# A weight block's low part: from a VectorE subtraction to ScalarE's negation and an accumulating DMA

## The chip, the cores and the metric

The kernel runs on one core of one Trainium2 chip. The metric is the device time of one execution in microseconds, the median of several runs. The core's engines are TensorE (PE in the profile; PEld is its weight load), VectorE (DVE), ScalarE (ACT), GpSimd (POOL) and SyncE (SP, which here only issues DMAs). Each engine works through its own queue in order and waits on semaphores for the others. A DMA that an engine issues stands in that engine's queue like any instruction: what it waits for holds back what is queued behind it.

## The reference

One inference step of a streaming encoder layer: an adaLN-modulated norm, an input projection, banded softmax attention beside an mLSTM memory, gated merge, output projection, and then a SwiGLU feed-forward network, for 1024 prompt rows and 32 sample rows together (1056 columns in the kernel's transposed layout). What matters here is the feed-forward part:

```python
    h2 = rmsnorm(x, g_ffn) * (1 + sc2) + sh2
    g, up = jnp.split(h2 @ w_gate_up, 2, axis=-1)
    x = x + gt2 * ((jax.nn.silu(g) * up) @ w_down)
```

with `D_MODEL = 1024` and `D_FF = 2816`, so `w_gate_up` is 1024 x 5632: 22 blocks of 128 gate columns and 22 of up columns.

## The kernel before

**Split numbers.** All large products are done in fp32r (a rounded fp32 that TensorE takes in one pass) with three passes per product: both operands are kept as a high part, the value rounded to fp32r, and a low part, the value minus its high part. `PASSES` multiplies high x high, low x high and high x low. A weight block's parts live in a tile of `wsplit_tile()`, named `wsp` in the profile, of shape 128 x 2 x 4 x 128: index 0 is the high part, index 1 the low part, 128 x 512 numbers (256 KB) each. There are four such tiles. `split_to` (lines 391 and 392 of the profile) makes both: ScalarE copies the source into the high part, VectorE subtracts that from the source into the low part.

**The weights' order.** `Weights` holds all blocks in the order of their use. Each `W.use(block)` first calls `advance`, which loads raw rows and splits blocks up to `self.ahead` past the block in use; in the stage of this case `W.ahead = 4`, and the four split tiles hold the block in use and the next three. So, ahead of the matmuls of block n, the splitting instructions of block n+3 are queued; its tile is the one that block n-1 has just left.

**Fifteen products.** The gate and up columns of feed-forward blocks 3 to 20 are 36 rows of 128 columns, taken three at a time: twelve "triples", each a `Fifteen`. A fast matrix multiplication scheme replaces the eighteen block products of a 3 x 2 by 2 x 3 product by fifteen. Each needs one weight block, which is one of the six raw blocks p, q, r, s, t, u of the triple (two in each of three raw 128 x 1024 rows), or a sum or difference of them. `block(dst, x, op, y)` describes one: its `make` forms the sum in place, over the raw block `dst` (or in an extra tile, `spare`). Blocks 1 to 4 (p, q, s, t) have no sum; the other eleven have one. `self.eng` is the engine that forms the sums: VectorE in the first triple, GpSimd in the eleven others (line 1367 of the profile). When block n is split, the sum of block n+1 is queued first, then the split of n, so that the sum is formed one block ahead:

```python
                self.block(x, r, minus, s, loads=(3,)),
                self.block(r, p, minus, r),
                self.block(u, q, minus, u),
                self.block(r, r, plus, s),
                self.block(u, t, plus, u),
```

These are blocks 5 to 9. Block 8 writes its sum over r, which is what block 6 was split from, and block 9 over u, which is what block 7 was split from; such a sum waits until the split has read it.

`times` issues a block's 12 matmuls (4 slices of the contraction x 3 passes) of 128 x 352 columns at line 1738. `fifteen_products` then adds the product to the rows that need it: the first time by ScalarE (line 1774), later by VectorE (line 1776). A completed third of a row is passed to `Act.complete`: SiLU by ScalarE (line 1801), the gate times up product by VectorE (line 1805), and a store of the finished block by SyncE (line 1807).

**Raw rows.** `load` (line 1352) has SyncE load a raw row of 512 KB into `wraw` (three buffers) or, for the third row of a triple, `raw` (one buffer). Such a load waits until everything that reads the old row is done.

Of the kernel before, what the change touches and what calls it, by code (L numbers as in the profile page):

```python
# [11 lines left out]
AF = mybir.ActivationFunctionType  # L12
ALU = mybir.AluOpType
# [126 lines left out]
def hybrid_stream_step(  # L140
# [11 lines left out]
    pe, act, dve, pool, sp = nc.tensor, nc.scalar, nc.vector, nc.gpsimd, nc.sync  # L152
# [25 lines left out]
    def slot(shape, dt=F32):  # L178
        return slots.tile(shape, dt, tag="s", name=nm("s"))
# [16 lines left out]
    def f(ap):  # L196
        return ap.bitcast(F32)
# [188 lines left out]
    def wsplit_tile():  # L386
        return wsp.tile([P, 2, 4, P], F32R, tag="wsp", name=nm("wsp"))

    def split_to(dst, src, eng=dve):

        act.activation(dst[:, 0], src, AF.Copy)  # L391
        eng.tensor_tensor(dst[:, 1], src, f(dst[:, 0]), op=ALU.subtract)  # L392
# [919 lines left out]
    class Fifteen:  # L1312
# [41 lines left out]
        def block(self, dst, x=None, op=None, y=None, loads=()):  # L1354
            def a(ij):
                return self.raw[ij[0]][:, 4 * ij[1]:4 * ij[1] + 4]

            def ld():
                for i in loads:
                    if i < 3:  # L1360
                        self.load(i)

            def make():
                if 3 in loads:
                    self.load(3)
                if op is not None:
                    self.eng.tensor_tensor(a(dst), a(x), a(y), op=op)  # L1367

            n = len(self.sums)
            self.sums.append(make)  # L1370

            def split(_):

                for f in self.sums[n + 1:n + 2]:
                    f()
                t = wsplit_tile()
                split_to(t, a(dst))
                return [t]
            return [ld, split, 1, None, 1]

# [292 lines left out]
    for pi, tiles in enumerate(parts):  # L1673
        if pi == 1:
            job = side.start(second_norm(parts[0]), 15, 50)
        for j in range(KD):
# [14 lines left out]
            a, b = tiles[0][0], tiles[-1][1]  # L1691
# [282 lines left out]
    for _ in range(3):  # L1974
        t = slot([P, 3, cut])
        cs += [t[:, i] for i in range(3)]
    for j in range(KD):
        wt = W.use(w_d0[j])
        n = 0
# [210 lines left out]
```

## Time and profile before

| | us |
|---|---|
| median of 3 runs | 1624.37 (1623.78 to 1625.40) |
| profiled execution | 1624.59 |
| its span | 1622.9 |
| TensorE busy in the span | 1586.7 (98%) |
| VectorE busy | 1123.9 (69%) |
| ScalarE busy | 782.9 (48%) |
| GpSimd busy | 434.7 (27%) |
| mean granted TensorE clock | 0.995 of full speed |

The profile counts an engine as busy while an instruction runs on its data path; issuing a DMA, waiting on a semaphore and branching are not counted. Groups of instructions are named by line, engine, operation, and the tiles written and read. "Idle before" is the time that the engine stood still ahead of the group, with what ended it. The triples that this case is about run from about 1020 to 1338 us of the span. Of the DMA queues, only SyncE's and ScalarE's carry transfers of the program in this kernel; GpSimd issues none.

### The profile page before, as it was taken

Reading aid. Unit: us, or ns where it says so; the run is one execution under the profiler, and the core shown is the slowest. Engines: PE = TensorE matmul, PEld = TensorE weight load, DVE = VectorE, ACT = ScalarE, POOL = GpSimd, SP = SyncE. Lnnn points to the kernel's source line nnn. Section 1 sums busy time; section 2 is a strip of 40 time slices with the busy share of each in tenths; the row PEclk is TensorE's granted clock in tenths of the full one; section 3 lists DMA queues with packets and bytes.
Section 4 is the critical chain, followed back from the end, with each engine's and each line's share of the span. In section 5 each row is a group of like instructions: output and inputs, shape, how many; then the busy total and the mean of one; then the engine's idle time right before and its main releaser. Section 6 shows DMA issues by size and latency. Waiting matters only on the chain.

```text
span 1622.9 us, 27478 instructions
## 1 busy us (share of the span) xinstructions
PE 1586.7 (98%) x10324; PEld 1567.1 (97%) x10324; DVE 1123.9 (69%) x2179; ACT 782.9 (48%) x1735; POOL 434.7 (27%) x462
## 2 busy tenths in 40 slices
PE   7989999999999999999999999999999999999997
PEld 6989999999999999999999999999999999999997
DVE  6756565546685845455654599989888886799754
ACT  3455454543455644444443465554544544545443
POOL 1233333434342311000011100556565550000001
PEclk9999999999999999999999999999999999999999
DMA  9722322332232333566443311323213227427454
GB/s 348 263 90 75 101 88 87 88 119 74 79 88 67 73 91 84 119 222 204 138 123 122 123 40 40 92 80 95 90 57 102 79 76 245 143 78 247 129 157 126
DMA packets 210327, 192.45 MB, mean 119 GB/s; under 512 B 10571, under 2 KB 180531, under 8 KB 209171
## 3 DMA queue, kind: packets, MB, share of 16 engines
q1 hardware_dynamic: 205354, 187.82, 37.0%
q10 hardware_dynamic: 4840, 2.88, 0.6%
q8 instruction: 81, 1.33, 0.3%
q14 instruction: 52, 0.42, 0.1%
HBM read 152.19 MB, written 41.63 MB: 119 GB/s over the span
## 4 chain that ended last, share of the span: by engine, by line
PE 90%; DVE 4%; ACT 2%; DMA 1%; issue 1%; POOL 0%; ACTq 0%; SPq 0%; DVEq 0%; POOLq 0%
PE mm L425 40%; PE psb L1738 18%; PE mm L1738 10%; PE mm L2141 3%; PE mm L830 3%; PE psb L2141 2%; PE psV L729 2%; PE psb L1984 2%; PE psS L671 1%; PE psT L698 1%; PE mm L1984 1%; PE psT L334 1%; PE mm L457 1%; DMA s<-in_x_prompt_dram 1%; DVE st L685 1%
## 5 line engine op out<-in xcount | busy, mean ns | idle before, releaser
L425 PE MATMUL mm<-s,wsp 128*128 128x352 f32 x4104 | 692.3, 325 | 2.1 <-DVE stg L515 1.6
L425 PEld LDWEIGHTS mm<-s,wsp 128*128 128x128 f32 x4104 | 659.7, 189 | 4.7 <-DVE stg L515 2.2
L392 DVE TENSOR_TENSOR wsp<-wraw,wsp 128x512 fp32r<-128x512 f32 (+1 forms) x284 | 237.4, 853 | 125.8 <-ACT wsp L391 123.7
L1738 PE MATMUL psb<-s,wsp 128*128 128x352 f32 x1611 | 271.7, 322 | 1.5 <-DVE wsp L392 0.8
L391 ACT ACTIVATE wsp<-wraw 128x512 fp32r<-128x512 f32 x340 | 201.8, 617 | 144.0 <-PE psb L1738 42.3
L1738 PEld LDWEIGHTS psb<-s,wsp 128*128 128x128 f32 x1611 | 260.5, 188 | 2.1 <-DVE wsp L392 1.1
L1738 PE MATMUL mm<-s,wsp 128*128 128x352 f32 x933 | 159.3, 322 | 0.0
L1738 PEld LDWEIGHTS mm<-s,wsp 128*128 128x128 f32 x933 | 151.2, 188 | 0.5 <-DVE wsp L392 0.5
L691 POOL TENSOR_SCALAR st<-st,mx 128x640 f32<-128x640 f32 (+5 forms) x72 | 55.6, 773 | 185.7 <-DVE mx L690 171.5
L1146 DVE SCALAR_TENSOR_TENSOR t<-wa,cmix,t 128x512 f32<-128x512 f32 x112 | 89.2, 801 | 12.3 <-DMA wa<-in_w_ada_dram 12.0
L392 POOL TENSOR_TENSOR wsp<-wraw,wsp 128x512 fp32r<-128x512 f32 x56 | 75.9, 1375 | 51.8 <-ACT wsp L391 51.4
L686 ACT ACTIVATE st<-st,mx 128x640 f32<-128x640 f32 (+5 forms) x72 | 47.9, 665 | 72.8 <-DVE mx L685 72.7
L685 DVE CUSTOM_DVE_ANT_0 st<-psS,bias 128x640 f32<-128x640 f32 (+5 forms) x72 | 44.4, 617 | 54.7 <-PE psS L671 41.4
L705 ACT ACTIVATE pT<-psT 128x640 fp32r<-128x640 f32 (+3 forms) x80 | 38.7, 493 | 70.0 <-PE psT L698 52.9
L1688 POOL TENSOR_TENSOR t<-t,sl 128x352 f32<-128x352 f32 x18 | 17.4, 966 | 185.3 <-ACT sl L1686 185.3
L2053 POOL TENSOR_TENSOR fst<-fst 128x1 f32<-128x1 f32 (+1 forms) x6 | 1.2, 192 | 236.6 <-ACT t L2046 236.6
L710 DVE TENSOR_TENSOR pT<-psT,pT 128x640 fp32r<-128x640 f32 (+3 forms) x80 | 44.0, 558 | 20.5 <-ACT pT L705 20.3
L1367 POOL TENSOR_TENSOR wraw<-wraw,raw 128x512 f32<-128x512 f32 x33 | 55.7, 1702 | 0.9
L830 PE MATMUL mm<-s,s 128*128 128x264 f32 (+3 forms) x432 | 54.9, 283 | 0.0
L2141 PE MATMUL mm<-s,wsp 128*128 128x352 f32 x330 | 54.4, 324 | 0.0
L2141 PEld LDWEIGHTS mm<-s,wsp 128*128 128x128 f32 x330 | 53.0, 188 | 0.0
L830 PEld LDWEIGHTS mm<-s,s 128*128 128x128 f32 (+1 forms) x432 | 51.9, 179 | 0.5
(380 smaller groups left out, 2511.5 us busy)
## 6 DMA issues: line engine op xcount, KB each, us to landing
wraw<-in_w_in_dram SPq DMA_DIRECT2D x40, 512.0 KB, 4.2
wraw<-in_w_gate_up_dram SPq DMA_DIRECT2D x33, 512.0 KB, 4.0
wa<-in_w_ada_dram SPq DMA_DIRECT2D x64, 256.0 KB, 4.1
wraw<-in_w_down_dram SPq DMA_DIRECT2D x32, 512.0 KB, 4.1
a_d<-t SPq DMA_DIRECT2D x22, 528.0 KB, 2.9
g_d<-t SPq DMA_DIRECT2D x16, 528.0 KB, 2.8
x<-xres SPq DMA_DIRECT2D x16, 528.0 KB
t<-g_d SPq DMA_DIRECT2D x16, 528.0 KB, 3.9
```

Of the source, the lines that this page charges most:

```text
L391: act.activation(dst[:, 0], src, AF.Copy)
L392: eng.tensor_tensor(dst[:, 1], src, f(dst[:, 0]), op=ALU.subtract)
L425: pe.matmul(pt[:, :hi - lo], wt[(w0 + k) // 4][:, a, (w0 + k) % 4], xt[k][:, b, lo:hi], start=(k == 0 and q == 0), stop=(k == n - 1 and q ...
L685: dve.tensor_tensor_reduce(so, sv, bi, -1.0, 3.0e38, ALU.add, ALU.min, mx[:n, 1:2])
L686: act.activation(st[:n, :w], st[:n, :w], AF.Exp, bias=mx[:n, 1:2], scale=-1.0, accum_out=mx[:n, 2:3])
L691: pool.tensor_scalar(st[:n, :w], st[:n, :w], mx[:n, 3:4], 1.0, op0=ALU.mult, op1=ALU.mult)
L830: pe.matmul(pt[:n, :wd], hs[k][:, a, i * P:i * P + n], whl[b][:, k, :wd], start=(k == 0 and q == 0), stop=(k == KD - 1 and q == 2))
L1146: dve.scalar_tensor_tensor(ac[:, c], wa, cmix[:, c, k:k + 1], ac[:, c], op0=ALU.mult, op1=ALU.add)
L1367: self.eng.tensor_tensor(a(dst), a(x), a(y), op=op)
L1738: pe.matmul(acc, wt[:, a, k], x[k][:, b], start=(start and not onto and k == 0 and q == 0), stop=(stop and k == 3 and q == 2), skip_group_ ...
L1984: pe.matmul(acc, wt[k // 4][:, u, k % 4], piece_of[k, i][:, v], start=(k == 0 and q == 0), stop=(k == KP - 1 and q == 2))
L2141: pe.matmul(acc, wt[(k - k0) // 4][:, u, (k - k0) % 4], piece_of[k, 2][:, v], start=(k == 0 and q == 0), stop=(k == NF - 1 and q == 2))
```

## The change

In the eleven triples whose sums GpSimd forms, the low part is made in another way. ScalarE copies the weights into the high part as before, then writes minus the high part into the low part's place. GpSimd issues a DMA whose source is the raw (or summed) block and whose destination is the low part, with `accum_op=ALU.add`: the DMA engines add the weights onto what stands there. The first triple keeps `split_to`. A loop variable is renamed so that `f`, which views an fp32r tile as fp32, can be used.

```diff
             def split(_):
 
-                for f in self.sums[n + 1:n + 2]:
-                    f()
+                for make in self.sums[n + 1:n + 2]:
+                    make()
                 t = wsplit_tile()
-                split_to(t, a(dst))
+                if self.eng is pool:
+
+                    act.activation(t[:, 0], a(dst), AF.Copy)
+                    act.activation(t[:, 1], t[:, 0], AF.Copy, scale=-1.0)
+                    pool.dma_start(f(t[:, 1]), a(dst), accum_op=ALU.add)
+                else:
+                    split_to(t, a(dst))
                 return [t]
             return [ld, split, 1, None, 1]
```

## The prediction

> **What bounds the kernel now.** I read the page first, then the stage that the change touches: the eleven triples whose sums GpSimd forms, about 1020 to 1338 us.
>
> ```profile
> span 1622.9 us, 27478 instructions
> ...
> PE 1586.7 (98%) x10324; PEld 1567.1 (97%) x10324; DVE 1123.9 (69%) x2179; ACT 782.9 (48%) x1735; POOL 434.7 (27%) x462
> ```
>
> The table of stretches says what holds in that stage (PE, PEld, DVE, ACT, POOL busy; then granted clock, DMA share, GB/s):
>
> ```profile
> core 0: us, PE busy (x) PEld busy (x) DVE busy (x) ACT busy (x) POOL busy (x), PEclk, DMA share, GB/s
> ...
> 1020.00:1338.00 318.00, 318.00 (x1983) 318.00 (x1982) 280.82 (x397) 157.53 (x306) 192.69 (x121) 1.00 0.26 83
> 1338.00:1400.00 62.00, 62.00 (x388) 62.00 (x387) 43.66 (x89) 31.76 (x75) 2.79 (x2) 1.00 0.68 225
> ```
>
> TensorE is never idle: 318.00/1983 = 0.160 us a matmul, 12 matmuls = 1.92 us a block, 15 blocks = 28.9 us a triple. The chain that ended last is TensorE alone from 1016.5 to beyond the stage's end:
>
> ```profile
> 1016.50 2.03 PE psb L1738 x11
> ...
> 1326.76 18.33 PE psb L1738 x114
> ```
>
> and of all of TensorE's waits those on these products lie in the first triple, ahead of 1016.5, which the change leaves alone:
>
> ```profile
> PE mm L1738 <- DVE x L1590: 1.1, 1, 1.1
> ...
> PE psb L1738 <- DVE wsp L392: 0.8, 1, 0.8
> PE psb L1738 <- ACT wsp L391: 0.7, 1, 0.7
> ```
>
> So VectorE, busy 280.82 of 318 us, bounds nothing here. What can move the time is only whether each block's low part is still there when TensorE wants it.
>
> **What is removed.** The groups of the stage (count | busy, mean ns | idle before):
>
> ```profile
> L392 DVE TENSOR_TENSOR wsp<-wraw,wsp 128x512 fp32r<-128x512 f32 x101 | 116.1, 1150 | 20.3 <-ACT wsp L391 19.0
> ...
> L391 ACT ACTIVATE wsp<-wraw 128x512 fp32r<-128x512 f32 x101 | 63.8, 632 | 68.3 <-PE psb L1738 26.5 <-POOL wraw L1367 19.9 <-PE mm L1738 16.1
> ...
> L392 DVE TENSOR_TENSOR wsp<-raw,wsp 128x512 fp32r<-128x512 f32 x44 | 44.3, 1008 | 5.2 <-ACT wsp L391 4.6
> ...
> L392 DVE TENSOR_TENSOR wsp<-spare,wsp 128x512 fp32r<-128x512 f32 x23 | 15.7, 681 | 1.9 <-ACT wsp L391 1.9
> ...
> L1774 ACT ACTIVATE t<-psb 128x352 f32<-128x352 f32 x45 | 19.3, 465 | 19.5 <-DVE t L1776 11.4 <-PE psb L1738 8.1
> ```
>
> VectorE loses 116.1 + 44.3 + 15.7 = 176 us of work (165 blocks, and three of the neighbours). TensorE waited for none of it, so I price the gain at nothing. One thing comes of it: GpSimd's sums get quicker (below).
>
> **What is added on ScalarE.** One more pass a block, 165 x 0.63 = 104 us, to 262 us of the stage: it still fits. Its place matters: high part and minus high part are queued behind the evacuations of the product before. A block is split three blocks ahead (four buffers, one in use), so from the release of its buffer to its use there are 3 x 1.92 = 5.76 us. Into that go at most two evacuations (0.94), the two passes (1.26), the DMA's issue I and its landing L. The window holds if I + L is below some 3.5 us; the values taken below, 3.6 together, stand just at its end.
>
> **What is added on GpSimd's queue.** No GpSimd DMA is in the trace, so both prices are bounded. For L, from the transfers that are there (KB, us from issue to landing):
>
> ```profile
> wraw<-in_w_gate_up_dram SPq DMA_DIRECT2D x33, 512.0 KB, 4.0
> wa<-in_w_ada_dram SPq DMA_DIRECT2D x64, 256.0 KB, 4.1
> ...
> a_d<-t SPq DMA_DIRECT2D x22, 528.0 KB, 2.9
> ...
> out_dram<-stg ACTq DMA_DIRECT2D x8, 256.0 KB, 2.2
> ```
>
> The nearest is the last: 256 KB read from on-chip memory, 2.2 us, of which the issue is 0.37 (next fence): 1.83 remain. An accumulating transfer reads a second stream of 256 KB; 272 KB more cost 2.9 - 2.2 = 0.7 us, so I take L = 1.83 + 0.67 = 2.5 us. Low end 1.83 (the second stream free), high end 4.1 - 0.37 + 0.67 = 4.4 us. For I, the time GpSimd's queue is held, the ends are an issue by SyncE and the longest pass of GpSimd over such a tile (ns, minimum, median, maximum):
>
> ```profile
> L1352 SPq DMA_DIRECT2D wraw<-in_w_gate_up_dram x25: 367/368/384, 923.6 to 1305.2; - x25
> ```
> ```profile
> L1367 POOL TENSOR_TENSOR raw<-raw x11: 1286/1292/1298, 1034.4 to 1322.5; 128x512 f32<-128x512 f32 x11
> L1367 POOL TENSOR_TENSOR raw<-wraw,wraw x11: 1813/1821/1827, 1037.5 to 1325.5; 128x512 f32<-128x512 f32 x11
> ```
>
> 0.37 to 1.82 us; no row is nearer to one end, so I take the middle, 1.1 us. A sum now takes 192.69/121 = 1.59 us; the 1.29 of the row above is reached where VectorE has no two-input subtraction beside it. With those gone I take 1.4 (ends 1.3 and 1.6).
>
> *GpSimd's throughput.* Eleven of a triple's fifteen blocks have a sum. There the queue needs 1.4 + 1.1 = 2.5 us a block, 0.58 over TensorE's pace. The four blocks without (1.1 us) let it get ahead, but no further than the window of three blocks, so I count seven of the steps at 2.5: 7 x 0.58 = 4.1 us a triple.
>
> *Two stalls in the queue.* Sums work in place. The eighth block's sum overwrites the operand that the sixth block's split reads, the ninth's that of the seventh. It shows in these two waits, eleven times each, and in one triple's order:
>
> ```profile
> POOL wraw L1367 <- DVE wsp L392: 70.8, 11, 7.6
> ...
> POOL raw L1367 <- DVE wsp L392: 6.9, 11, 0.6
> ```
> ```profile
> 1059.76 0.69 DVE L392 TENSOR_TENSOR wsp<-wraw,wsp 128x512 fp32r<-128x512 f32 x1 [1.40 <-ACT wsp L391]
> ...
> 1060.53 1.29 POOL L1367 TENSOR_TENSOR wraw<-wraw 128x512 f32<-128x512 f32 x1 [6.53 <-DVE wsp L392]
> ...
> 1061.37 1.00 DVE L392 TENSOR_TENSOR wsp<-raw,wsp 128x512 fp32r<-128x512 f32 x1 [0.92 <-ACT wsp L391]
> ...
> 1062.45 1.29 POOL L1367 TENSOR_TENSOR raw<-raw 128x512 f32<-128x512 f32 x1 [0.63 <-DVE wsp L392]
> ```
>
> Now the reader is the DMA issued on the very queue that waits: a split queues the next block's sum and then its own DMA, so the order is DMA 6, sum 8, DMA 7, sum 9, DMA 8. Sum 8 stands until DMA 6 has landed; DMA 7 is queued behind sum 8; sum 9 stands until DMA 7 has landed, with DMA 8 behind it. ScalarE's high parts of blocks 8 and 9 wait for those sums as well. Twice a step is sum + issue + landing + some 0.1 of hand-over = 1.4 + 1.1 + 2.5 + 0.1 = 5.1 us instead of 1.92: 2 x 3.18 = 6.4 us a triple.
>
> *Other queues.* SyncE's reload of a raw row waited for VectorE's last read and now waits for a landing. The tightest: block 13 landed, then 4.0 us of load, 1.26 of ScalarE and 3.6 of DMA = 8.9 us, against five blocks (9.6 us) until the next triple's third block: hidden by 0.7 us, and 11 x the excess if I + L passes 4.3. The 165 transfers ride beside a DMA share of 0.26; a 512 KB load in the way is inside the high end of L.
>
> **The sum.** (4.1 + 6.4) x 11 = 115 us onto the profiled execution's 1624.59 us (span 1622.9, 1.7 around it; the median of the runs is 1624.37, 0.2 less): 1740 us. A measurement of this kernel tells about 0.2%, 3.2 us, from no change.
>
> The Trainium skill, "DMA: Bandwidth & Descriptors", section "Anatomy of one DMA", puts a GpSimd-issued DMA at 2.0 us plus bytes over 436 GB/s, issue included: an estimate of 2.6 us for 256 KB, not counting a second stream. With 2.6 for I + L the stalls would be 2 x 2.18 = 4.4 us a triple and the result 1718. No run yet shows which is nearer.
>
> **Rivals.**
>
> *Hidden (not slower), 1624.6 us.* The place is the two stalls. From the end of the second block the chain for the eighth is 0.94 + 1.26 + 3(I + L) + 2 sums of 1.3, and 9.6 us are there: below I + L of about 1.6 us nothing is lost, and the issue must be under 0.6 us for the other steps. The fastest transfer above, 2.2 us with its issue, speaks against it. Nor would it be faster: TensorE has no idle time here, and from 88% VectorE load (280.82/318) to 70% (43.66/62) its matmul goes only from 0.160 to 0.160 us (62.00/388).
>
> *Cheap issue.* I = 0.37: no loss of throughput, and two steps of 1.4 + 0.37 + 2.5 + 0.1 = 4.4: 2 x 2.45 x 11 = 54 us, 1678; with L = 1.83 and sums of 1.3 it is 2 x 1.68 x 11 = 37 us, 1661. For it: two queues issue at that price; against it, neither is GpSimd's.
>
> *Slow transfer or issue.* I = 1.82 with L = 2.5: steps of 5.8 and 3.2, 2 x 3.9 + 7 x 1.3 = 16.9, and the window overrun by 0.94 + 1.26 + 4.3 - 5.76 = 0.75 over three blocks, 1 us over four: 17.9 x 11 = 197, 1822. I = 1.1 with L = 4.4: 2 x 5.1 + 4.1 + 2.6 = 16.9 x 11 = 186, 1810. Both at their ends would give some 1890.
>
> *The clock.* Stalls of 3.2 us could cost TensorE its clock. After short waits early in the kernel the granted clock was 0.64:
>
> ```profile
> 48.00:52.00 4.00, 3.51 (x14) 3.18 (x15) 4.00 (x8) 2.62 (x6) 0.00 (x0) 0.64 1.03 415
> ```
>
> That is 0.36 x 4 = 1.4 us lost. Once a triple beside the stalls: 11 x 1.4 = 16 us more, 1756. Against it, part of the slow matmuls would lie inside the waits. By the Trainium skill ("TensorE: Matmul & The Clock Gate", "What's actually happening") the clock halves after an idle window of about 3.4 us; the row agrees that waits cost clock, and whether 3.2 us with a block between does is open.
>
> **How the numbers follow.** Forecast (both stalls and a GpSimd-paced middle, 1680 to 1800): 0.60. Cheap issue: 0.15. Slow: 0.14. Clock: 0.07. Hidden: 0.03. Faster, by something that this stage doesn't show: 0.01. The range goes from the cheap end, 1661, to 1850, above each slow case alone (1822) and below both together (1890); outside lie the hidden case and parts of the cheap and slow ones, under 0.2. Slower 0.96, same 0.03, faster 0.01.
>
> **What would show it.** In the changed profile: VectorE's subtractions of the stage gone and its load near a quarter ((281 - 176)/433); ScalarE near 60%; the stage some 115 us longer, TensorE's matmuls waiting for DMA into the split tiles, most in two gaps of about 3 us a triple; sums eight and nine waiting for a DMA, and GpSimd the queue that the other gaps go back to. Gaps spread evenly over all blocks would say that L, not the queue, paces. No gaps would say that I + L is under 1.6 us, and a longer stage without gaps that the clock fell. The prediction is wrong if a GpSimd issue costs far from 1.1 us, or if the accumulation runs at another rate than a copy.

## The result and the profile after

The changed kernel takes 1748.53 us (median of four, 1747.86 to 1753.76) against 1624.86: ratio 1.0768, 95% interval 1.0753 to 1.0783. The forecast was 1740, the range 1661 to 1850. The profiled execution took 1747.86 us, its span is 122.0 us longer. In the page (third line: packets, MB and share of the sixteen DMA engines of the queue that GpSimd issues to):

```profile
span 1744.9 us, 27922 instructions
...
PE 1631.7 (94%) x10324; PEld 1586.8 (91%) x10324; DVE 984.5 (56%) x2014; ACT 884.6 (51%) x1900; POOL 540.1 (31%) x627
...
q0 software_dynamic: 23760, 43.26, 14.6%
```

The stage of the eleven triples in the table of stretches, in the same columns as before the change:

```profile
1016.00:1460.00 444.00, 367.30 (x2010) 341.41 (x2011) 147.03 (x240) 261.24 (x475) 298.02 (x287) 0.95 0.76 157
```

It ends near 1460 instead of 1338 us: all of the loss lies here. TensorE stands still for 444.00 - 367.30 = 77 us where it was never idle. The other 45 us are longer busy time: 367.30/2010 = 0.183 us a matmul instead of 0.160, at a granted clock of 0.95. VectorE went from 88% to 33%; the DMA engines from a share of 0.26 to 0.76. What TensorE waits for (us in total, times, longest):

```profile
PE psb L1744 <- DMA wsp<-wraw: 34.1, 37, 2.4
PE mm L1744 <- DMA wsp<-wraw: 21.8, 19, 2.8
PE psb L1744 <- DMA wsp<-raw: 12.0, 7, 2.4
...
PE mm L1744 <- DMA wsp<-raw: 8.6, 7, 2.4
```

Each of these waits ends with the landing of an accumulating DMA. GpSimd's queue in one triple, by the timeline (start, duration, and idle time before with its end):

```profile
1072.49 0.86 POOL L1381 DMA_DIRECT2D wsp<-wraw  x1 [0.24 <-POOL raw L1367]
1075.86 1.28 POOL L1367 TENSOR_TENSOR wraw<-wraw 128x512 f32<-128x512 f32 x1 [2.50 <-DMA wsp<-wraw]
1077.09 0.87 POOL L1381 DMA_DIRECT2D wsp<-raw  x1
1080.42 1.28 POOL L1367 TENSOR_TENSOR raw<-raw 128x512 f32<-128x512 f32 x1 [2.47 <-DMA wsp<-raw]
1081.66 0.87 POOL L1381 DMA_DIRECT2D wsp<-wraw  x1
1082.27 1.56 POOL L1367 TENSOR_TENSOR wraw<-wraw,raw 128x512 f32<-128x512 f32 x1
1083.67 1.00 POOL L1381 DMA_DIRECT2D wsp<-raw  x1
1084.28 1.72 POOL L1367 TENSOR_TENSOR raw<-wraw,wraw 128x512 f32<-128x512 f32 x1
1085.56 1.26 POOL L1381 DMA_DIRECT2D wsp<-wraw  x1
...
1093.08 1.60 POOL L1367 TENSOR_TENSOR wraw<-wraw 128x512 f32<-128x512 f32 x1
```

This is the order that the prediction wrote down: DMA 6, sum 8, DMA 7, sum 9, DMA 8. Each of the two sums stands idle until the DMA just ahead of it has landed, and the steps are 4.60 (1072.49 to 1077.09) and 4.57 us. Behind them issue and sum alternate at 2.01 and 1.89 us, then somewhat more: the six steps from the ninth sum to the last take 12.66 us here (1080.42 to 1093.08) and 12.63 in the mean of the eleven triples, 2.11 a step. Note that a sum starts 0.61 us after an issue, while the issue's row is 0.87 long or more: the two overlap.

From one eighth sum to the next a triple takes (1396.55 - 1036.28)/9 = 40.0 us, before (1320.34 - 1032.29)/10 = 28.8. The 11.2 us are 2 x 2.66 = 5.3 for the two stalled steps, 6 x 0.19 = 1.1 for GpSimd's pace, and about 5 that lie in the eight steps from a triple's last sum to the next triple's eighth. One of these eight is the first stalled step, which is counted above; for the other seven the prediction had counted next to nothing.

### The profile page after: what moved, and what is told of

The parts are those of the page before. It is cut to its first block, busy times and chain, and to the rows that moved or that the text cites. A ratio compares the mean times of both kernels' runs of the same rounds, so it can differ in the third digit from the quotient of the medians.

```text
span 1744.9 us, 27922 instructions
## 1 busy us (share of the span) xinstructions
PE 1631.7 (94%) x10324; PEld 1586.8 (91%) x10324; DVE 984.5 (56%) x2014; ACT 884.6 (51%) x1900; POOL 540.1 (31%) x627
## 4 chain that ended last, share of the span: by engine, by line
PE 71%; DMA 9%; issue 6%; ACT 5%; POOL 5%; DVE 4%; ACTq 0%; POOLq 0%; SPq 0%; DVEq 0%
PE mm L425 37%; PE psb L1744 8%; DMA wsp<-wraw 7%; PE mm L1744 5%; PE mm L2147 3%; PE mm L830 2%; PE psb L2147 2%; POOL wraw L1367 2%; PE psV L729 2%; PE psb L1990 2%; POOL raw L1367 1%; PE psS L671 1%; ACT wsp L1379 1%; POOL wsp L1381 1%; PE psT L698 1%
## 5 line engine op out<-in xcount | busy, mean ns | idle before, releaser
L425 PE MATMUL mm<-s,wsp 128*128 128x352 f32 x4104 | 692.0, 325 | 2.1 <-DVE stg L515 1.6
L425 PEld LDWEIGHTS mm<-s,wsp 128*128 128x128 f32 x4104 | 659.4, 189 | 4.7 <-DVE stg L515 2.2
L1744 PE MATMUL psb<-s,wsp 128*128 128x352 f32 x1611 | 296.5, 334 | 48.6 <-DMA wsp<-wraw 34.1
L1744 PE MATMUL mm<-s,wsp 128*128 128x352 f32 x933 | 177.8, 340 | 30.5 <-DMA wsp<-wraw 21.8
L1744 PEld LDWEIGHTS mm<-s,wsp 128*128 128x128 f32 x933 | 159.9, 199 | 40.3 <-DMA wsp<-wraw 28.1
L392 DVE TENSOR_TENSOR wsp<-wraw,wsp 128x512 fp32r<-128x512 f32 (+1 forms) x185 | 122.8, 690 | 104.4 <-ACT wsp L391 103.8
L391 ACT ACTIVATE wsp<-wraw 128x512 fp32r<-128x512 f32 (+1 forms) x241 | 139.2, 611 | 77.4 <-PE mm L2147 21.1
L1381 POOL DMA_DIRECT2D wsp<-wraw x99 | 92.3, 933 | 172.2 <-PE mm L1744 100.5
L1782 DVE TENSOR_TENSOR t<-t,psb 128x352 f32<-128x352 f32 x77 | 39.3, 520 | 127.6 <-PE psb L1744 127.4
L1379 ACT ACTIVATE wsp<-wraw 128x512 fp32r<-128x512 f32 x99 | 62.5, 631 | 95.2 <-POOL wraw L1367 48.0
L1380 ACT ACTIVATE wsp<-wsp 128x512 fp32r<-128x512 f32 x165 | 104.2, 632 | 5.2
L1782 DVE TENSOR_TENSOR t<-t,mm 128x352 f32<-128x352 f32 x43 | 22.1, 520 | 84.7 <-PE mm L1744 84.7
```

Source lines behind the costliest of these rows:

```text
L425: pe.matmul(pt[:, :hi - lo], wt[(w0 + k) // 4][:, a, (w0 + k) % 4], xt[k][:, b, lo:hi], start=(k == 0 and q == 0), stop=(k == n - 1 and q ...
L1379: act.activation(t[:, 0], a(dst), AF.Copy)
L1380: act.activation(t[:, 1], t[:, 0], AF.Copy, scale=-1.0)
L1381: pool.dma_start(f(t[:, 1]), a(dst), accum_op=ALU.add)
L1744: pe.matmul(acc, wt[:, a, k], x[k][:, b], start=(start and not onto and k == 0 and q == 0), stop=(stop and k == 3 and q == 2), skip_group_ ...
L1782: dve.tensor_tensor(c, c, y, op=ALU.add if sign > 0 else ALU.subtract)
```

## The experiments

All edits are to the changed kernel, in the eleven triples; times are medians, ratios to the kernel before on the same chip with their 95% intervals.

| run | us | ratio |
|---|---|---|
| blocks 6, 7 by VectorE | 1700.4 | 1.0461 (1.0444 to 1.0479) |
| blocks 10, 12 by VectorE | 1746.3 | 1.0746 (1.0730 to 1.0762) |
| block 13 by VectorE | 1737.4 | 1.0690 (1.0675 to 1.0706) |
| blocks 6, 7, 13 by VectorE | 1680.0 | 1.0340 (1.0325 to 1.0356) |
| VectorE adds, no DMA | 1628.1 | 1.0020 (1.0011 to 1.0030) |
| plain DMA | 1692.6 | 1.0421 (1.0403 to 1.0439) |
| sums on VectorE | 1710.9 | 1.0527 (1.0511 to 1.0543) |
| sums, and blocks 6, 7, 13, on VectorE | 1666.1 | 1.0258 (1.0233 to 1.0283) |
| the same with plain DMA | 1637.0 | 1.0075 (1.0058 to 1.0091) |
| only blocks 1 to 5 by DMA | 1642.5 | 1.0118 (1.0097 to 1.0139) |
| only blocks 8 to 12, 14, 15 by DMA | 1641.0 | 1.0100 (1.0085 to 1.0115) |
| gaps filled with matmuls | 1748.7 | 1.0768 (1.0750 to 1.0786) |

**The two stalls.** Blocks are counted from 0 in the code, from 1 in the text.

```diff
-                if self.eng is pool:
+                if self.eng is pool and n not in (5, 6):
```

> Blocks 6 and 7 of each of the eleven triples get their low part from VectorE again, so that sums 8 and 9 wait for a subtraction and not for a landing; the other thirteen keep the accumulating DMA. Theory A (the two stalls in GpSimd's queue are the largest part): the changed profile has steps of 4.6 us there instead of 1.92, 2 x 2.65 x 11 = 58 us, and after the second of them the granted clock is 0.84 over 10 us, 1.6 x 11 = 18 us; without them about 1748 - 58 to 76 = 1672 to 1690, and no wait of a GpSimd sum for a DMA. Rival B (every DMA costs alike: the length of the path to the landing or GpSimd's load paces all blocks): 2 of 15 DMAs fewer take 2/15 of the 124 us, 17 us: about 1731.

Its control has `(9, 11)` in that place:

> The control for the run beside it: blocks 10 and 12, which no sum right behind overwrites, get their low part from VectorE. Theory A: both stalls stay; GpSimd is spared two issues of 0.6 us in the stretch where it sets the pace by 0.17 us a block, so 0 to 11 us less: 1737 to 1748. Rival B: as much as for blocks 6 and 7, about 1731.

Two DMAs fewer take 48 us off where a sum waits for them, and 2, within the intervals, where none does. That speaks for theory A and against rival B: it is not the number of DMAs, it is the two that a sum waits for. But 1700 also lies outside theory A's 1672 to 1690: the gain is 10 us short of the 58 that the steps promised, and nothing of the 18 for the clock shows.

**The late reload**, `(12,)` in that place, and both together, `(5, 6, 12)`:

> Block 13 alone gets its low part from VectorE: it is the last reader of the first raw row, whose buffer the next triple's second row is loaded into. Theory C (the reload is late): ScalarE waited 24 us in ten times for that load in the changed profile, and five steps from the last sum of a triple to the first of the next take 11.8 us instead of 9.6; reading done 3 us earlier takes 2.2 x 11 = 24 us off: about 1724. If the load is not what is waited for at that place, only an issue goes, 0 to 7 us: 1741 to 1748.

> The three blocks together. Theories A and C both: 58 to 76 us and 24 us off, 1648 to 1666. If one of them holds alone, the time of that run alone. Rival B: 3/15 of 124 us, 1723.

Block 13 alone gives 11 us, half of what theory C said and more than an issue; with the stalls gone it gives 20 (1700 to 1680). So the reload is one of the waits, partly covered by the others. Both theories together promised 1648 to 1666; 1680 is above that. In the run of the three blocks the two sums wait for VectorE, as in the kernel before, 0.9 us in the mean:

```profile
1069.32 1.29 POOL L1367 TENSOR_TENSOR wraw<-wraw 128x512 f32<-128x512 f32 x1 [1.23 <-DVE wsp L392]
1071.24 1.30 POOL L1367 TENSOR_TENSOR raw<-raw 128x512 f32<-128x512 f32 x1 [0.63 <-DVE wsp L392]
1072.86 0.88 POOL L1381 DMA_DIRECT2D wsp<-wraw  x1 [0.32 <-POOL raw L1367]
```

**ScalarE's second pass alone.**

```diff
-                    pool.dma_start(f(t[:, 1]), a(dst), accum_op=ALU.add)
+                    dve.tensor_tensor(t[:, 1], a(dst), f(t[:, 1]), op=ALU.add)
```

> One part alone: ScalarE's second pass stays, and VectorE adds the weights onto the negated high part in place of the DMA (a VectorE pass as before the change). Prediction: the extra 0.63 us of ScalarE a block lies in the window of 5.76 us and costs nothing: 1624.4, within 3 us. Rival: ScalarE's queue (evacuations behind two passes) paces the blocks: 1640 or more.

It costs 3.3 us, interval 1.8 to 4.9: a little above the 3 us that "nothing" allowed, and far from the rival's 1640. All but these 3 of the 124 us come with the DMA.

**The price of the accumulation.** `accum_op=ALU.add` is left away:

> The same DMA without the addition: it copies the weights over the negated high part, so the low part is not formed (left out: the accumulation). Queue, waits and bytes written stay. If the second stream and the addition cost the 0.67 us of the prediction, each of the two stalled steps is 0.67 us shorter, and the landings in the other blocks too: 15 to 40 us less than the changed kernel's 1748, 1708 to 1733. If accumulation runs at a copy's rate, 1748.

56 us less, more than either line allowed. In GpSimd's timeline a triple takes 35.5 us there instead of 40.0. The two stalled steps are 3.59 us each in the triple below (1068.07 to 1071.66 to 1075.25):

```profile
1068.07 0.56 POOL L1381 DMA_DIRECT2D wsp<-wraw  x1 [0.84 <-POOL raw L1367]
1070.44 1.28 POOL L1367 TENSOR_TENSOR wraw<-wraw 128x512 f32<-128x512 f32 x1 [1.81 <-DMA wsp<-wraw]
1071.66 0.56 POOL L1381 DMA_DIRECT2D wsp<-raw  x1
1074.02 1.28 POOL L1367 TENSOR_TENSOR raw<-raw 128x512 f32<-128x512 f32 x1 [1.79 <-DMA wsp<-raw]
1075.25 0.55 POOL L1381 DMA_DIRECT2D wsp<-wraw  x1
```

In the mean of the eleven triples the two steps together are 2.1 us shorter, the six steps behind them 1.0 (11.66 us, 1.94 a step), and the rest of the triple 1.5. The landings of the DMA, issue included, in the changed kernel and here (us, minimum, median, maximum):

```profile
DMA to landing us min/median/max: 3.2/3.9/7.0
```

```profile
DMA to landing us min/median/max: 2.2/2.6/6.6
```

The addition costs 1.0 us undisturbed and 1.3 in the median. And the queue's line over the stage (changed kernel 444 us, 165 DMAs; plain 370 us, 156 DMAs):

```profile
q0 software_dynamic: 23616, 43.00, 57.1%
```

```profile
q0 software_dynamic: 12408, 40.67, 29.7%
```

0.571 x 444/165 = 1.54 us of all sixteen engines for one accumulating 256 KB, 0.297 x 370/156 = 0.70 for a plain one. The runs below with fewer such DMAs give 1.54 to 1.58 and 0.73 in the same way. One accumulating DMA every 1.92 us would take 80% of the engines; with the 0.26 that was there before they would be full. That is an estimate for TensorE's old pace; at the pace that the stage has, the share is 0.76. GpSimd gains as well, by the groups of the plain run (count | busy, mean ns):

```profile
L1381 POOL DMA_DIRECT2D wsp<-wraw x99 | 54.7, 552 | 175.4 <-PE mm L1744 96.7 <-ACT wsp L1380 25.6 <-ACT t L1807 20.6
L1367 POOL TENSOR_TENSOR wraw<-wraw,raw 128x512 f32<-128x512 f32 x33 | 42.8, 1297 | 0.7
```

against the same groups of the changed kernel:

```profile
L1381 POOL DMA_DIRECT2D wsp<-wraw x99 | 92.3, 933 | 172.2 <-PE mm L1744 100.5 <-ACT wsp L1380 27.3 <-ACT t L1807 19.2
L1367 POOL TENSOR_TENSOR wraw<-wraw,raw 128x512 f32<-128x512 f32 x33 | 60.1, 1820 | 0.0
```

**The sums on VectorE.**

```diff
-                    self.eng.tensor_tensor(a(dst), a(x), a(y), op=op)
+                    dve.tensor_tensor(a(dst), a(x), a(y), op=op)
```

> All eleven triples' sums on VectorE (0.69 us each, it is free for 76% of the stage); GpSimd only issues the accumulating DMAs. Sums 8 and 9 still wait for a landing, but DMA 7 no longer stands behind sum 8. Theory A (what costs is that the wait stands in the queue that issues the DMAs): the two landings overlap, the chain from block 2's end to block 8's start is 0.94 + 1.26 + 3.4 + 0.7 + 1.26 + 3.4 = 11.0 us against 9.6, some 1.4 us a triple, and no GpSimd pace: 1640 to 1665. Rival F (what costs is the landing itself, wherever the wait stands): two serial landings again, 2 x (0.7 + 3.4 + 0.1 - 1.92) = 4.6 us a triple, and the late reload 2.2: 1700.

1711: near rival F's 1700, not theory A's 1640 to 1665. (In the changed kernel VectorE was free for 67% of the stage; the 76% came from the prediction.) Taking the sums out of GpSimd's queue gave 38 us; it moved the wait and did not remove it:

```profile
DVE wraw L1367 <- DMA wsp<-wraw: 44.3, 9, 7.0
```

What stands behind it in VectorE's queue now are the additions of the products, and behind those ScalarE's passes. So it costs that a sum waits for a landing in an in-order queue, in this queue or that. With blocks 6, 7 and 13 subtracted by VectorE besides:

> Sums on VectorE, and blocks 6, 7 and 13 with VectorE's subtraction: no wait of a sum for a landing, no early reader of the first raw row, no sum in GpSimd's queue. Against the run with the three blocks alone (1680, 55 us over the kernel before). Theory D (those 55 us are GpSimd's pace, sum and issue 2.1 us a block): all of it goes, 1625 to 1632. Rival E (they are landings of 4 us and more at the end of a window that holds 3.5): most stays, 1660 or more.

1666, 14 us below the run of the three blocks alone: about GpSimd's pace (1.1 x 11 = 12 us by the steps above). Theory D falls, and rival E's "1660 or more" holds; 42 us are left. TensorE waits for landings again, 27 us in all, here the longest:

```profile
1065.91 2.04 PE L1744 MATMUL psb<-s,wsp 128*128 128x352 f32 x11 [2.90 <-DMA wsp<-wraw]
```

The stretches around it (DMA share and GB/s last) show the DMA engines full just there, with a row load and two stores beside the accumulation:

```profile
1060.00:1064.00 4.00, 3.01 (x19) 2.72 (x18) 3.23 (x7) 2.87 (x7) 1.50 (x2) 1.00 1.03 331
1064.00:1068.00 4.00, 2.09 (x13) 2.10 (x14) 1.40 (x3) 0.80 (x3) 0.23 (x1) 1.00 1.05 230
```

By the Trainium skill ("DMA: Bandwidth & Descriptors", "Issuing engines are not separate DMA queues") DMAs of all issuing engines share the same sixteen; the trace agrees: in the changed kernel's stage a 512 KB row load of SyncE's lands in 5.7 us instead of 4.1.

**What is left.** The last run with the accumulation left away, and the accumulation in a part of the blocks only:

> The last run (sums on VectorE; blocks 6, 7, 13 subtracted there; 1666) with plain DMAs for the other twelve: the low part is not formed (left out: the accumulation). Theory G (what is left, 42 us, is the DMA engines' time: an accumulating 256 KB takes 0.571 x 444 / 165 = 1.54 us of all sixteen in the changed kernel, a plain one 0.297 x 370 / 156 = 0.70): nearly all goes, 1625 to 1633. Rival H (the path ScalarE, GpSimd, landing is too long for the window even undisturbed): a landing shorter by 1.0 of 3.2 us takes at most a third to a half of it, 1645 or more.

> Sums on VectorE; only blocks 1 to 5 of a triple by the accumulating DMA, which is when SyncE's two or three row loads and the stores run; the other ten by VectorE's subtraction. Theory G: the waits of twelve accumulating blocks (42 us) lie where loads and stores run too, and stay for the most part: 1645 to 1660. Rival (every accumulating DMA costs alike): 5/12 of 42, 17 us: 1642.

> The complement: sums on VectorE; blocks 8 to 12, 14 and 15 by the accumulating DMA, where little else is moved; the others by VectorE's subtraction. Theory G: few waits, 1625 to 1635. Rival: 7/12 of 42, 24 us: 1649.

The plain copy takes 29 of the 42 us (1637), between theory G and rival H and nearer to G: the accumulation is most of what was left; of the 12 us that remain, some 3 are ScalarE's pass. The two partial runs cost 17 us for five blocks and 16 for seven. Early blocks are dearer each (3.5 against 2.3 us), but the first run came out as the rival said and the second between the two. The late blocks were not the quiet place that I took them for: of TensorE's fifteen waits for them, ten are for block 14, in the tile of its own, which is issued just as the next triple's row loads start (the largest groups):

```profile
PE psb L1744 <- DMA wsp<-spare: 4.0, 7, 1.4
PE mm L1744 <- DMA wsp<-spare: 2.7, 3, 1.5
PE psb L1744 <- DMA wsp<-wraw: 2.1, 4, 0.9
```

How the 29 us divide between longer landings and engines that are simply full stays open.

**The clock.** The changed kernel's granted clock fell to 0.65 around a stall:

```profile
1119.00:1122.00 3.00, 2.35 (x9) 2.36 (x10) 0.00 (x0) 0.99 (x2) 2.32 (x3) 0.66 0.03 5
1122.00:1124.00 2.00, 1.28 (x5) 0.83 (x3) 0.52 (x1) 1.49 (x4) 2.00 (x3) 0.65 0.76 131
```

TensorE's gaps there were 1.14, 1.92 and 0.93 us within 16 us:

```profile
1109.77 7.95 PE L1744 MATMUL mm<-s,wsp 128*128 128x352 f32 x48 [1.14 <-DMA wsp<-wraw]
1119.64 3.35 PE L1744 MATMUL mm<-s,wsp 128*128 128x352 f32 x11 [1.92 <-DMA wsp<-raw]
1122.79 0.50 PE L1744 MATMUL psb<-s,wsp 128*128 128x352 f32 x1
1124.21 3.23 PE L1744 MATMUL psb<-s,wsp 128*128 128x352 f32 x17 [0.93 <-DMA wsp<-wraw]
```

To see what this costs, the next run fills the gaps with matmuls whose result nothing reads:

```diff
+            if x.eng is pool and r in (6, 2):
+                acc = bank()
+                for i in range(12):
+                    pe.matmul(acc, FORMS[r][i % 4][:, 0, :P], FORMS[r][i % 4][:, 0], start=(i == 0), stop=(i == 11))
             if r in ONTO:
```

> The changed kernel with 12 more matmuls ahead of block 7 and 12 ahead of block 8 of each of the eleven triples, into a PSUM bank that nothing reads: 1.92 us of TensorE work in each of the two gaps of the stalls (added work, the output is not touched by it). The queues, the sums and the DMAs are those of the changed kernel. Theory K (the stalls also cost TensorE's clock: granted 0.65 to 0.72 over 3 to 6 us a triple, 1.2 to 1.7 us, and the matmuls behind the stall are what the next blocks wait for): TensorE stays warm and the time falls by 13 to 18 us, to 1730 to 1735. Rival (the slow matmuls lie beside GpSimd's queue, which sets the pace there anyway): 1748, within 4 us; above 1752 if the added matmuls don't fit the gaps.

The stage's clock rises from 0.95 to 0.99 with 264 matmuls more, and the time stays:

```profile
1016.00:1462.00 446.00, 395.03 (x2288) 367.97 (x2288) 139.98 (x245) 263.38 (x479) 298.15 (x287) 0.99 0.76 157
```

GpSimd's steps are the same 4.6 us. So the clock cost nothing that can be seen, which fits slow matmuls that lay beside the queue that set the pace. The run adds 264 x 0.160 = 42 us of matmuls and takes only some 29 us off TensorE's waits, so a gain by the clock that the added work used up is not excluded by it alone. The run without the two stalls speaks against such a gain: there the clock is at 0.99 again, and it still saved less than the steps promised.

## Why the prediction was right

**Sign and bound: right.** TensorE was never idle in the stage before, so relieving VectorE had nothing to give. VectorE's load came to 33% and not near a quarter: the durations of its groups overlap (before the change they add up to 304 us in a busy time of 280.82), so taking off 176 us was too much.

**The two stalls: right in place and order, a fifth too large.** Two steps of 4.6 us instead of 5.1. The sum (1.28 against 1.4), and issue and landing (3.3 against 3.6) were each a little below the estimate. The run without them gives 48 us back of the predicted 6.4 x 11 = 70; the steps hold 58, and the other waits presumably close in over the rest.

**GpSimd's pace: right in kind, four times too large.** 0.19 us over TensorE's pace in six steps, not 0.58 in seven; 1.1 us a triple instead of 4.1; where the sums leave GpSimd's queue, with the stalls gone, 14 us instead of 45. The failed number is I = 1.1: the middle of two far ends. The next sum starts 0.61 us after an issue. The sum does get longer beside it, 1.6 to 1.95 us where I took 1.4, yet the pair is 2.1 and not 2.5.

**"SyncE's reload ... hidden by 0.7 us": wrong.** It was worked out with a load of 4.0 us and a landing of 3.6. Beside the accumulations the load takes 5.7 and the landing 3.9 in the median, up to 7.0. The step that failed is the sentence that the DMAs "ride beside a DMA share of 0.26": the bytes of the new DMAs were counted in the landing and not in the engines' time, 1.54 us each. The runs show 11 to 20 us of loss as the reload.

**The window of three blocks: put at nothing, and it was not.** The prediction had it hold up to an I + L of 3.5 us, took 3.6 and added no term for it. Issue and landing were 3.9 us in the median and up to 7.0. The run that has neither the stalls, nor the early reader of the first raw row, nor a sum on GpSimd is still 42 us above the kernel before, 3 of them ScalarE's pass.

Reload and window are what the record shows for the 5 us a triple that the sum did not have. With the accumulation left away in the changed kernel 1.5 of the 5 go, so the addition, by its engine time or its later landing, is a part of it; how the rest divides stays open.

So the nearness of 1740 to 1748.5 is luck: two terms were too large by 1.1 and 3.0 us a triple, and about 5 us were missing. What was right is the sign, the place of the stalls and their size within a fifth.

**The extra ScalarE pass, put at nothing: 3.3 us** in the run that isolates it.

**L = 2.5, with 0.67 us for a second stream.** The plain DMA from GpSimd landed in 2.2 us at best, as the store that I took it from; the addition costs 1.0 and not 0.67. The Trainium skill's 2.6 us for 256 KB ("DMA: Bandwidth & Descriptors", "Anatomy of one DMA"), an estimate without a second stream, is the plain DMA's median here; for an accumulating one it is too little, and the 1718 that it led to was too low.

**The rivals.** Hidden: excluded, its point was an I + L of 1.6 and the fastest landing is 3.2. Cheap issue: half true; the next sum started 0.61 us after an issue, but the time did not follow, since the sums beside an issue got longer and the reload and the window cost what this rival did not count. Slow: not by its causes, as neither an I of 1.82 nor, in the median, an L of 4.4 came about, but its overrun of the window did. Clock: the clock did fall, around gaps of 0.9 to 2.4 us, and it cost nothing that could be measured. The Trainium skill ("TensorE: Matmul & The Clock Gate", "What's actually happening") names an idle window of about 3.4 us; these gaps were shorter.

No version here beats the kernel before: in this stage it has no idle time of TensorE to give.

## What to carry to other kernels

An engine at 88% beside one that is never idle is no reason to move its work: look at which wait ends last before relieving anybody. When a compute step becomes a DMA, whoever overwrites its source waits for a landing and no longer for a pass of 0.7 us, and if that waiter stands in the queue that issues the next DMA, the landings become serial; list the in-place writers first. Moving the waiter to another engine's queue gave back 38 of the 124 us here, leaving its two readers a pass gave 48. And price the DMA engines by their time, not by bytes alone.

## What the runs showed of the hardware that was not expected

- An accumulating DMA of 256 KB on chip kept the sixteen DMA engines for 1.54 us each in the mean, a plain one for 0.70, and landed 1.0 us later (3.2 against 2.2 at best).
- On GpSimd the next instruction started 0.56 to 0.63 us after the issue of an accumulating DMA, whose row lasts 0.84 to 1.27 us, and a two-input pass beside it took 1.6 to 1.95 us; beside plain DMAs (issue 0.55) the same passes took 1.30.
- TensorE's granted clock fell to 0.65 around gaps of 1 to 2 us that came close together. One gap of 2.90 us, in the run with the sums and three blocks on VectorE (1064 to 1068 us), left it at 1.00.
